# FFN output product of a decoder block: more chunk pairs by seven products, with some of their factors kept in DRAM

## The chip, the cores and the metric

The kernel runs on one core of one Trainium2 chip. The metric is the device time of one execution in microseconds (us). Three runs of the kernel before took 2199.93, 2201.72 and 2203.13 us, so the median is 2201.72 us.

## The reference, cut to what matters

One decoder block on 512 tokens of width 2048 in fp32: an attention mixer (`nsa_mixer`), then a SwiGLU FFN with 5632 hidden columns, then a final RMSNorm. The change touches the last product of the FFN and its neighbours only:

```
def swiglu(h, w_in, w_out):
    z = h @ w_in
    a, b = z[..., :D_FF], z[..., D_FF:]
    return (jax.nn.silu(a) * b) @ w_out
...
        h = h + swiglu(rmsnorm(h, ffn_norm_g[i]), ffn_w_in[i], ffn_w_out[i])
    return rmsnorm(h, final_norm_g)
```

Call `silu(a) * b` the activation A (512 x 5632) and `ffn_w_out` the weights B (5632 x 2048). The kernel computes A B.

## The kernel before, in words

Every fp32 product is made of three matmuls (`three`, L267 to L270): both factors are split into a high part, rounded to the matmul's format, and a low rest. The high part is written by ScalarE (ACT) and the rest by VectorE (DVE); the products high-high, high-low and low-high are accumulated in PSUM.

**The FFN output stage.** The inner dimension 5632 is cut into 22 chunk pairs of 256 (j = 0 to 21) and the 2048 output columns into four blocks of 512 (b = 0 to 3). One step of the stage, a *visit*, is one chunk pair in one block: 4 x 22 = 88 visits, numbered n = 0 to 87 in the order of `ORDER[b]`, block after block. A visit needs the activation of the pair (512 KB, written to DRAM as `d_a` by the stage before) and a 256 x 512 tile of the weights (512 KB).

- A **plain** visit (`plain_tile`) makes 4 token tiles x 2 chunks x 3 = 24 matmuls with 512 columns. It needs the activation loaded (`load_a`) and split (`split_a`) and the weights split.
- A **seven** visit (`seven_unit`) treats the pair as a 2 x 2 block product by seven products (Winograd's form of Strassen's method) instead of eight: 7 products x 2 x 3 = 42 matmuls with 256 columns. On the activation side it needs seven factors (p1 to p7, 128 x 1792 in a high and a low tile, `ah` and `al`, 917,504 bytes each). On the weight side it needs three sums of weight quarters (`weight_sums`: four subtractions or additions on DVE, then a split of 128 x 768).

Before, seven of the 22 pairs are seven visits in every block. Their activation factors are made by `form` at their first visit (in block 0) and stay in SBUF in the pool `asl` for all four blocks. `form` reads the activation from `scratch`, the last quarter of the accumulator `acc`, which is free until block 3. SyncE (SP) loads the next pair to form into it (`load_form`); after the last form, a GpSimd (POOL) DMA puts the residual from `d_r` there.

Four of the seven sums of a block (p1, p5, p6, p7) have PSUM banks of their own (`qs`) and are merged into `acc` by `merge_sums` after the last seven visit of the block.

**What sets the order.** The schedule is manual: each engine executes its instructions in program order. In the loop over visits, iteration n issues, in this order: `prepare(n + 1)` (a form, if visit n + 1 needs one), `W2.take` (the weights of visit n + 1 are split, with the sums if it is a seven visit), `split_a` (the activation of visit n + 1, if plain), the matmuls of visit n, `merge_sums` where due, and one step of `ready`. So DVE does the whole preparation of visit n + 1 in one row. It can't run far ahead: the tiles `thi`/`tlo` (split activation of a plain visit, or split weight sums of a seven visit) have two buffers, so the one for visit n + 1 is free when visit n - 1 has ended on TensorE (PE). The weights have three raw buffers (`RAW`) and four split buffers (`CONV`). The raw activations of plain visits have two single homes, `rawx` and `tt`; `tt` also takes the weight sums.

`ready(b)` runs in block b + 1: at its third visit it issues the load of a 512-column piece of the final norm's gain (`gf`, one buffer, a POOL DMA), and at the next four visits one multiplication of `acc` with `gf` each, on DVE.

The last four visits of block 3 (`N_TAIL`) are done token tile by token tile: all four visits for tile 0, then for tile 1, and so on, with the final norm and the output store behind each tile. Their split activations go to buffers of `asl`, as those come free.

SP's queue carries the loads of weights, of plain activations and of pairs to form; POOL's queue carries `gf` and the loads of `d_r` in this stage.

Of the kernel before, what the change touches and what calls it, by code (L numbers as in the profile page):

```python
# [165 lines left out]
def nsa_block(ctx: ExitStack, tc: tile.TileContext, x, rel_bias, mix_g, ffn_g, fin_g, w_in, w_out,  # L166
# [919 lines left out]
    NU = len(seq)  # L1086
    a_raw, a_hl, seven = {}, {}, {}


    held, free = {}, {"rawx": -1, "tt": -1}  # L1090
    for n, (_, j) in enumerate(seq):
        home = "tt"
        if j not in SEVEN:
            home = min(free, key=free.get)
            held[n] = home, free[home]
        free[home] = n
# [9 lines left out]
    def split_a(n):  # L1106
# [8 lines left out]
        elif n < NU:  # L1115
            a_hl[n] = seven[seq[n][1]]
        load_a(n)
# [3 lines left out]
    def weight_sums(n):  # L1121

        def first(r):
            b11, b12, b21, b22 = (r[:, 256 * i:256 * (i + 1)] for i in range(4))
            ttf = tp.tile([128, 1536], F32, name="tt", bufs=1)[:, :768]
            tt = ttf.rearrange("p (n c) -> p n c", n=3)
            sub(tt[:, 0], b22, b12)
# [4 lines left out]
            def rest():  # L1132
                h, l = (tp.tile([128, 1600], F32R, name=f"t{x}")[:, 32:800] for x in ("hi", "lo"))
                act(h, ttf, AF.Copy)
                sub(l, ttf, f32(h))
                t_hl[n] = [x.rearrange("p (n c) -> p n c", n=3) for x in (h, l)]
# [4 lines left out]

    for n, (_, j) in enumerate(seq):
        if j in SEVEN:
            W2.sums[n] = weight_sums(n)
# [19 lines left out]
    late.tile([128, 16], F32, name="late_gap")  # L1164
    asl = ctx.enter_context(tc.tile_pool(name="asl", bufs=len(SEVEN)))
    late2 = ctx.enter_context(tc.tile_pool(name="late2", bufs=1))
    ss = [late2.tile([128, 4], F32, name=f"sf{t}") for t in range(NT)]
    scratch = acc[:, :, 1536:]
    forms = [j for _, j in seq[:NF // 2] if j in SEVEN]

    def load_form(i):
        if i < len(forms):
            nc.sync.dma_start(scratch[:, :2], d_a[forms[i]].rearrange("p (n c) -> p n c", n=2))
        else:
            pool.dma_start(scratch, d_r[:, :, 1536:].rearrange("t p c -> p t c"))

    def form(j):
# [9 lines left out]
        for c0, c1, src in ((0, 256, a11), (256, 768, a[:, 1]), (768, 1792, m)):  # L1187
# [4 lines left out]
            sub(ol, src, f32(oh))  # L1192
        seven[j] = [x.rearrange("p (n c) -> p n c", n=7) for x in (h, l)]

# [3 lines left out]
    def prepare(n):  # L1198

        j = seq[n][1] if n < NU else None  # L1200
        if n < NF // 2 and j in SEVEN:
            form(j)
            load_form(forms.index(j) + 1)

# [54 lines left out]
    for b in range(4):  # L1259
        units = ORDER[b][:-N_TAIL] if b == 3 else ORDER[b]  # L1260
        po = [pf.tile([128, 512], F32, name=f"f{i}") for i in range(4)]
        qs = {x: pf.tile([128, 512], F32, name=f"f{i}") for i, x in enumerate(("p1", "p5", "p6", "p7"))}
        first7 = next(j for j in units if j in SEVEN)
        last7 = [j for j in units if j in SEVEN][-1]
        started = False
        for i, j in enumerate(units):
# [3 lines left out]
            while na <= n + 1 + max(0, 2 - left):  # L1270
                split_a(na)
                na += 1
            if j in SEVEN:
                seven_unit(n, w, first7)
# [65 lines left out]
```

## Time and profile before

| quantity | value |
|---|---|
| the profiled execution's own time | 2201.19 us |
| its span (first to last instruction) | 2199.4 us |
| median of three runs | 2201.72 us (2199.93 to 2203.13) |
| mean granted TensorE clock | 0.997 |
| PE, PEld, DVE, ACT, POOL busy | 98%, 90%, 69%, 42%, 4% |
| FFN output stage on PE | 1719.6 to 2189.7 us |
| DMA traffic of the whole span | 306.34 MB, mean 139 GB/s |
| seven visits, plain visits | 28, 60 |

How to read it: the profile is one execution, 1.8 us shorter in span than its device time. Busy shares are of the span; PEld is the loading of the stationary operand, beside PE. Window rows of the trace give, for a stretch of the span, the busy time of each engine with its number of instructions in brackets, the granted TensorE clock (1.00 is full), the mean busy share of the 16 DMA engines, and GB/s. In rows of the timeline the columns are start, duration, engine, line, operation, tiles, shape and count; in square brackets stands how long the engine sat idle before it and what released it. Rows of DMA issues give the count, the size and the median us from issue to landing. q1 is the hardware queue that SP's loads use, q0 the software queue of POOL.

### The profile page before, as it was taken

The page shows a single profiled execution, that of the slowest core. Times are in us where ns is not written, and L with a number is a line of the kernel's source. Part 1 is how long each engine was busy: PE and PEld are TensorE (multiplying, and loading weights), DVE is VectorE, ACT ScalarE, POOL GpSimd, SP SyncE. Part 2 cuts the span into 40 slices and gives each one's busy share as a digit, 9 for nine tenths or more (in the row PEclk, how much of TensorE's full clock was granted, in tenths as well). Part 3 has the DMA queues.
Part 4 walks back from the last instruction along what each step waited for, and adds up shares of the span by engine and source line. Part 5 has one row for each costly group of instructions (what it writes and reads, how often), then busy time and mean ns, then how long its engine had stood idle before and what let it go on. Part 6 is the DMA issues. An engine that isn't in the chain of part 4 may idle for free.

```text
span 2199.4 us, 36466 instructions
## 1 busy us (share of the span) xinstructions
PE 2158.3 (98%) x14866; PEld 1990.0 (90%) x14866; DVE 1523.9 (69%) x2458; ACT 929.0 (42%) x1429; POOL 97.4 (4%) x95
## 2 busy tenths in 40 slices
PE   6999999999999999999999999999999999999998
PEld 5889898888989888899999999999999888888886
DVE  5454656656655437798888888888888678566665
ACT  5343444444444324343434434343444344344344
POOL 3100000000013012000000000000000000000000
PEclk9999999999999999999999999999999999999999
DMA  5755233323253543244444334333443655555445
GB/s 167 206 147 158 81 93 91 92 82 97 89 204 115 187 149 116 96 134 126 125 125 134 122 120 125 127 122 126 126 125 125 223 199 196 179 173 166 162 158 182
DMA packets 233496, 306.34 MB, mean 139 GB/s; under 512 B 12367, under 2 KB 178287, under 8 KB 232176
## 3 DMA queue, kind: packets, MB, share of 16 engines
q1 hardware_dynamic: 226016, 273.58, 38.9%
q0 software_dynamic: 6016, 27.29, 3.4%
q10 hardware_dynamic: 1296, 3.15, 0.4%
q8 instruction: 116, 1.90, 0.3%
q14 instruction: 52, 0.43, 0.1%
HBM read 275.56 MB, written 33.66 MB: 141 GB/s over the span
## 4 chain that ended last, share of the span: by engine, by line
PE 94%; DVE 3%; DMA 1%; ACT 1%; issue 0%; SPq 0%; ACTq 0%; DVEq 0%
PE f L269 19%; PE f L268 18%; PE f L270 18%; PE proj L268 8%; PE proj L270 8%; PE proj L269 8%; PE pt L735 2%; PE pp L270 1%; PE pp L269 1%; PE pp L268 1%; PE o L270 1%; PE o L269 1%; PE s L268 1%; PE s L270 1%; PE o L268 1%; PE s L269 1%
## 5 line engine op out<-in xcount | busy, mean ns | idle before, releaser
L92 DVE TENSOR_TENSOR wlo<-raw,whi 128x1024 fp32r<-128x1024 f32 (+1 forms) x208 | 252.5, 1217 | 136.8 <-ACT whi L90 135.9
L90 ACT ACTIVATE whi<-raw 128x1024 fp32r<-128x1024 f32 (+1 forms) x226 | 234.0, 1039 | 156.7 <-DVE raw L890 62.9
L890 DVE TENSOR_TENSOR tlo<-tt,thi 128x1536 fp32r<-128x1536 f32 (+2 forms) x132 | 197.8, 1498 | 141.6 <-ACT thi L992 89.0
L268 PE MATMUL f<-hn_h,whi 128*128 128x256 f32 x984 | 271.7, 276 | 0.7 <-ACT E L950 0.7
L270 PE MATMUL f<-hn_h,wlo 128*128 128x256 f32 x984 | 271.6, 276 | 0.0
L269 PE MATMUL f<-hn_l,whi 128*128 128x256 f32 x984 | 271.6, 276 | 0.0
L987 ACT ACTIVATE whi<-raw 128x1024 fp32r<-128x1024 f32 x123 | 126.1, 1057 | 292.4 <-DVE raw L890 282.1
L268 PE MATMUL proj<-hn_h,whi 128*128 128x512 f32 (+1 forms) x544 | 210.2, 386 | 1.0 <-DVE hn_l L257 1.0
L270 PE MATMUL proj<-hn_h,wlo 128*128 128x512 f32 (+1 forms) x544 | 207.6, 382 | 0.0
L269 PE MATMUL proj<-hn_l,whi 128*128 128x512 f32 (+1 forms) x544 | 207.1, 381 | 0.0
L268 PEld LDWEIGHTS f<-hn_h,whi 128*128 128x128 f32 x984 | 184.7, 188 | 1.1 <-ACT E L950 1.1
L270 PEld LDWEIGHTS f<-hn_h,wlo 128*128 128x128 f32 x984 | 184.7, 188 | 0.0
L269 PEld LDWEIGHTS f<-hn_l,whi 128*128 128x128 f32 x984 | 184.7, 188 | 0.0
L270 PE MATMUL f<-whi,tlo 128*128 128x512 f32 x448 | 175.1, 391 | 1.2 <-DVE tlo L890 1.2
L269 PE MATMUL f<-wlo,thi 128*128 128x512 f32 x448 | 174.9, 390 | 0.0
L268 PE MATMUL f<-whi,thi 128*128 128x512 f32 x448 | 174.6, 390 | 0.0
L992 ACT ACTIVATE thi<-tt 128x1536 fp32r<-128x1536 f32 x82 | 121.8, 1485 | 84.6 <-PE f L269 75.9
L890 DVE TENSOR_TENSOR wlo<-raw,whi 128x1024 fp32r<-128x1024 f32 x123 | 147.0, 1223 | 0.0
L268 PE MATMUL proj<-whi,hn_h 128*128 128x256 f32 (+2 forms) x496 | 146.3, 295 | 0.0
L269 PE MATMUL proj<-wlo,hn_h 128*128 128x256 f32 (+2 forms) x496 | 145.2, 293 | 0.0
L270 PE MATMUL proj<-whi,hn_l 128*128 128x256 f32 (+2 forms) x496 | 145.0, 292 | 0.0
L294 DVE TENSOR_TENSOR ptl<-pt,pth 128x128 fp32r<-128x128 f32 (+3 forms) x128 | 62.4, 488 | 99.1 <-ACT pth L293 98.9
(314 smaller groups left out, 5894.1 us busy)
## 6 DMA issues: line engine op xcount, KB each, us to landing
raw<-in_ffn_w_in SPq DMA_DIRECT2D x135, 512.0 KB, 3.6
raw<-in_ffn_w_out SPq DMA_DIRECT2D x88, 512.0 KB, 4.5
raw<-in_nsa_w_in SPq DMA_DIRECT2D x48, 512.0 KB, 3.6
rawx<-in_ffn_w_in SPq DMA_DIRECT2D x41, 512.0 KB, 4.9
rawx<-d_a SPq DMA_DIRECT2D x36, 512.0 KB, 3.6
raw<-in_nsa_w_out SPq DMA_DIRECT2D x32, 512.0 KB, 3.6
raw<-in_nsa_w_in SPq DMA_DIRECT2D x56, 256.0 KB, 3.3
tt<-d_a SPq DMA_DIRECT2D x24, 512.0 KB, 4.5
```

The costliest lines, as they stand in the source:

```text
L90: self.nc.scalar.activation(hi[:, :n], src, AF.Copy)
L92: eng.tensor_tensor(lo[:, :n], src, hi[:, :n].bitcast(F32), op=OP.subtract)
L268: mm(o, ah, bh, start=start, stop=False, skip_group_check=True)
L269: mm(o, ah, bl, start=False, stop=False, skip_group_check=True)
L270: mm(o, al, bh, start=False, stop=stop, skip_group_check=True)
L294: dve.tensor_tensor(lo, psum_ap, hi.bitcast(F32), op=OP.subtract)
L735: nc.tensor.transpose(pt[rows, 128 * (t - kt):128 * (t - kt + 1)], src, ident)
L890: dve.tensor_tensor(o, a, b, op=OP.subtract)
L987: act(h, r, AF.Copy)
L992: act(h, ttf, AF.Copy)
```

## The change

The set of seven visits now depends on the block. Five pairs, `KEPT` = 3, 8, 13, 17, 19, are seven visits everywhere and keep their factors in SBUF (`asl`, now five buffers of a high and a low tile). Nine more pairs become seven visits from some block on: 5, 10, 15 from block 0; 0, 1, 2, 4 from block 1; 6, 7 from block 2. Their factors are formed once, in a new pool `ast` with two buffers, and used from there; `form` also writes them to DRAM (`d_s`, two POOL DMAs). In each later block they are loaded back into a buffer of `ast` (`load_seven`, two POOL DMAs per visit). In total 48 visits are seven and 40 are plain; 14 pairs are formed, where 7 were.

The visits of the four blocks, numbered n:chunk pair, with p for plain, k for kept, v for passing through `ast`, f where the pair is formed:

```
0:0p 1:1p 2:2p 3:3fk 4:4p 5:5fv 6:6p 7:7p 8:8fk 9:9p 10:10fv 11:11p 12:12p 13:13fk 14:14p 15:15fv 16:16p 17:17fk 18:18p 19:19fk 20:20p 21:21p
22:3k 23:6p 24:5v 25:7p 26:0fv 27:9p 28:8k 29:11p 30:10v 31:12p 32:1fv 33:14p 34:13k 35:16p 36:2fv 37:17k 38:15v 39:18p 40:4fv 41:19k 42:20p 43:21p
44:5v 45:9p 46:3k 47:10v 48:11p 49:6fv 50:12p 51:15v 52:8k 53:14p 54:0v 55:16p 56:13k 57:1v 58:18p 59:7fv 60:17k 61:2v 62:19k 63:4v 64:20p 65:21p
66:5v 67:3k 68:10v 69:9p 70:15v 71:8k 72:0v 73:11p 74:1v 75:13k 76:2v 77:12p 78:4v 79:17k 80:6v 81:19k 82:7v 83:14p 84:16p 85:18p 86:20p 87:21p
```

In the program, the load for a visit stands in the iteration in which its buffer's user is at work, and POOL waits there until that user has ended on PE. From block 2's end on this is two v visits earlier: the load for visit 72 waits for the end of visit 68, and so on to visit 82, which waits for 78. The loads for visits 38, 51 and 61 stand in iterations 35, 48 and 58, right behind a form and its two writes. The last form is that of visit 59, so the load of the residual into `scratch` is now issued in iteration 58 too, between the writes of that form and the load for visit 61. In block 3 the `gf` load is issued in iteration 68, behind the load for visit 72.

The tail's four plain visits now follow only one plain visit (83) after the last seven visit (82), and `merge_sums` of block 3 is issued in iteration 82. Before, five plain visits stood between.

The core of the diff:

```diff
-SEVEN = (3, 6, 9, 12, 14, 17, 19)
-ORDER = [tuple(range(22))] + 2 * [(3, 0, 1, 6, 2, 4, 9, 5, 7, 12, 8, 10, 14, 11, 13, 17, 15, 16, 19, 18, 20, 21)] + [
-    (3, 0, 6, 1, 9, 2, 12, 4, 14, 5, 17, 7, 19, 8, 10, 11, 13, 15, 16, 18, 20, 21)]
+KEPT = (3, 8, 13, 17, 19)
+SEVEN = [KEPT + x for x in ((5, 10, 15), (5, 10, 15, 0, 1, 2, 4)) + 2 * ((5, 10, 15, 0, 1, 2, 4, 6, 7),)]
+ORDER = [tuple(range(22)),
+         (3, 6, 5, 7, 0, 9, 8, 11, 10, 12, 1, 14, 13, 16, 2, 17, 15, 18, 4, 19, 20, 21),
+         (5, 9, 3, 10, 11, 6, 12, 15, 8, 14, 0, 16, 13, 1, 18, 7, 17, 2, 19, 4, 20, 21),
+         (5, 3, 10, 9, 15, 8, 0, 11, 1, 13, 2, 12, 4, 17, 6, 19, 7, 14, 16, 18, 20, 21)]
...
+    d_s = dram.tile([NF // 2, 2, 128, 1792], F32, name="d_s")
...
-            a_hl[n] = seven[seq[n][1]]
+            a_hl[n] = seven[seq[n][1]] if seq[n][1] in KEPT else passing.pop(0)
...
+            c0 = 0 if n and seq[n - 1][1] in SEVEN[seq[n - 1][0]] else 32
...
-                h, l = (tp.tile([128, 1600], F32R, name=f"t{x}")[:, 32:800] for x in ("hi", "lo"))
+                h, l = (tp.tile([128, 1600], F32R, name=f"t{x}")[:, c0:c0 + 768] for x in ("hi", "lo"))
...
-    asl = ctx.enter_context(tc.tile_pool(name="asl", bufs=len(SEVEN)))
+    asl = ctx.enter_context(tc.tile_pool(name="asl", bufs=len(KEPT)))
+    ast = ctx.enter_context(tc.tile_pool(name="ast", bufs=2))
...
-    forms = [j for _, j in seq[:NF // 2] if j in SEVEN]
+    forms = [n for n, (b, j) in enumerate(seq) if j in SEVEN[b] and (not b or j not in SEVEN[b - 1])]
+    visits = [n for n, (b, j) in enumerate(seq) if j in SEVEN[b] and j not in KEPT]
...
-        h, l = (asl.tile([128, 1792], F32R, name=f"a{x}") for x in "hl")
+        h, l = ((asl if j in KEPT else ast).tile([128, 1792], F32R, name=f"a{x}") for x in "hl")
...
+        if j not in KEPT:
+            for i, x in enumerate((h, l)):
+                pool.dma_start(d_s[j, i], x.bitcast(F32))
+        keep_seven(j, h, l)
...
+    def load_seven(n):
+
+        while n_visit[0] < len(visits):
+            v = visits[n_visit[0]]
+            if v in forms or sum(x > n for x in visits[:n_visit[0]]) >= 2:
+                break
+            h, l = (ast.tile([128, 1792], F32R, name=f"a{x}") for x in "hl")
+            for i, x in enumerate((h, l)):
+                pool.dma_start(x.bitcast(F32), d_s[seq[v][1], i])
+            keep_seven(seq[v][1], h, l)
+            n_visit[0] += 1
...
+        if n in forms:
+            form(seq[n][1])
+            load_form(forms.index(n) + 1)
+            n_visit[0] += n in visits
...
+            load_seven(n)
             if i >= 2:
                 next(todo, None)
```

More of the change, by code (lines that the diff above doesn't have):

```diff
@@ L1086, in nsa_block @@
     NU = len(seq)
-    a_raw, a_hl, seven = {}, {}, {}
+    a_raw, a_hl, seven, passing = {}, {}, {}, []
     held, free = {}, {"rawx": -1, "tt": -1}
-    for n, (_, j) in enumerate(seq):
+    for n, (b, j) in enumerate(seq):
         home = "tt"
-        if j not in SEVEN:
+        if j not in SEVEN[b]:
             home = min(free, key=free.get)
@@ L1140, in weight_sums @@
         return first
-    for n, (_, j) in enumerate(seq):
-        if j in SEVEN:
+    for n, (b, j) in enumerate(seq):
+        if j in SEVEN[b]:
             W2.sums[n] = weight_sums(n)
@@ L1192, in form, with keep_seven @@
             sub(ol, src, f32(oh))
-        seven[j] = [x.rearrange("p (n c) -> p n c", n=7) for x in (h, l)]
+        if j not in KEPT:
+            for i, x in enumerate((h, l)):
+                pool.dma_start(d_s[j, i], x.bitcast(F32))
+        keep_seven(j, h, l)
+    def keep_seven(j, h, l):
+        x = [x.rearrange("p (n c) -> p n c", n=7) for x in (h, l)]
+        if j in KEPT:
+            seven[j] = x
+        else:
+            passing.append(x)
+    n_visit = [0]
+    def load_seven(n):
[8 more added lines that the diff above has]
+            n_visit[0] += 1
     pool.dma_start(acc[:, :, :1536], d_r[:, :, :1536].rearrange("t p c -> p t c"))
@@ L1198, in prepare @@
     def prepare(n):
[L1200 to L1203, printed above, removed]
+        if n in forms:
+            form(seq[n][1])
+            load_form(forms.index(n) + 1)
+            n_visit[0] += n in visits
     def plain_tile(n, w, t, first, last):
@@ L1262, in nsa_block @@
         qs = {x: pf.tile([128, 512], F32, name=f"f{i}") for i, x in enumerate(("p1", "p5", "p6", "p7"))}
-        first7 = next(j for j in units if j in SEVEN)
-        last7 = [j for j in units if j in SEVEN][-1]
+        first7 = next(j for j in units if j in SEVEN[b])
+        last7 = [j for j in units if j in SEVEN[b]][-1]
         started = False
```

4 lines of the change are left out of this document (2 added, 2 removed).

## The prediction, on record before the run

> **What bounds the kernel now.** First the page, then the chain of waits, then the stage by windows.
>
> ```profile
> span 2199.4 us, 36466 instructions
> PE 2158.3 (98%) x14866; PEld 1990.0 (90%) x14866; DVE 1523.9 (69%) x2458; ACT 929.0 (42%) x1429; POOL 97.4 (4%) x95
> PE 94%; DVE 3%; DMA 1%; ACT 1%; issue 0%; SPq 0%; ACTq 0%; DVEq 0%
> 1720.00:1740.00 20.00, 19.36 (x97) 16.00 (x97) 16.66 (x24) 8.85 (x11) 1.28 (x2) 1.00 0.83 311
> 1740.00:1760.00 20.00, 17.50 (x90) 14.56 (x89) 14.20 (x19) 9.59 (x11) 0.00 (x0) 0.94 0.61 221
> 1760.00:2140.00 380.00, 380.00 (x2215) 335.70 (x2214) 254.28 (x327) 160.59 (x187) 2.94 (x5) 1.00 0.53 178
> 1754.97 0.38 PE L268 MATMUL f<-thi,ah 128*128 128x256 f32 x1 [0.96 <-ACT thi L1134]
> 1756.37 0.38 PE L269 MATMUL f<-tlo,ah 128*128 128x256 f32 x1 [1.01 <-DVE tlo L890]
> 1758.00:1762.00 4.00, 4.00 (x24) 4.00 (x24) 1.72 (x2) 0.00 (x0) 0.00 (x0) 0.60 0.86 288
> ```
>
> PE is the bound, 94% of the chain. In the output stage it is idle for 0.64 and 2.50 us in the first 40 us and then works 380 of 380 us. DMA stands at 178 GB/s there. One thing to remember: after two waits of about 1 us at 1755, the granted clock was 0.60 over the next 4 us, which costs about 4 x 0.4 = 1.6 us more.
>
> **The gain on PE.** Exact windows of one seven visit and of two plain ones:
>
> ```profile
> 1841.71:1846.56 4.85, 4.85 (x43) 1.00 0.76 242
> 1846.56:1857.49 10.93, 10.93 (x51) 1.00 0.63 208
> 1650.00:1700.00 50.00, 50.00 (x443) 50.00 (x442) 44.70 (x53) 20.90 (x20) 1.07 (x2) 1.00 0.39 127
> ```
>
> A seven visit takes 4.85 us, a plain one 10.93 / 2 = 5.465. The change turns 20 plain visits into seven visits: 20 x 0.615 = **-12.3 us**. Seven visits in a row (block 3) cost no more: in the stage before, 443 matmuls of 256 columns ran in 50 us, 0.113 us each, against 4.85 / 42 = 0.115 here.
>
> **What DVE gets.** One preparation with form, one without:
>
> ```profile
> 1816.70 1.23 DVE L890 TENSOR_TENSOR tlo<-rawx,thi 128x1024 fp32r<-128x1024 f32 x1 [0.22 <-ACT thi L1112]
> 1817.85 0.42 DVE L893 TENSOR_TENSOR acc<-acc 128x256 f32<-128x256 f32 x1
> 1821.67 0.42 DVE L890 TENSOR_TENSOR tt<-raw 128x256 f32<-128x256 f32 x1
> 1824.82 0.95 DVE L890 TENSOR_TENSOR tlo<-tt,thi 128x768 fp32r<-128x768 f32 x1
> 1836.47 0.42 DVE L890 TENSOR_TENSOR tt<-raw 128x256 f32<-128x256 f32 x1
> 1839.63 0.95 DVE L890 TENSOR_TENSOR tlo<-tt,thi 128x768 fp32r<-128x768 f32 x1
> L1254 DVE TENSOR_TENSOR acc<-acc,gf x12: 683/684/686, 1859.7 to 2106.7; 128x512 f32<-128x512 f32 x12
> ```
>
> A form takes 1817.85 to 1821.67 = 3.8 us, the weights of a seven visit 1836.47 to 1840.58 = 4.1, a plain preparation two splits of about 1.15, a `gf` step 0.68. Seven visits in a row need 4.1 (4.8 with a `gf` step) of 4.85 us: hidden. For seven, plain, formed seven, the plain split ends 2.3 us after the first seven visit s starts (its `thi` is free only then: 1815.6 to 1817.9), so the formed one is ready at s + 2.3 + 3.8 + 4.1 = 10.2, and PE wants it at 10.3. Fits by 0.1 us; every lateness shows. Visit 49 has a `gf` step ahead of its form: 0.6 us late. Forms 15 and 17 stand two visits apart while 15's factors are being written; the scratch load has 10.3 - 3.8 = 6.5 us, I take 0.5 late (0 to 1.5). The start of block 0 (form 5 where form 6 was) waits for the same 3 MB load; I take no difference (-4 to +4, its whole loss on either side). The shifted column `c0` changes no shape: nothing, to 0.1 us each way.
>
> **What DMA gets.**
>
> ```profile
> 1730.00:1734.00 4.00, 4.00 (x19) 3.30 (x19) 3.74 (x8) 1.67 (x2) 0.00 (x0) 1.00 1.02 415
> 1738.00:1742.00 4.00, 4.00 (x36) 3.89 (x34) 0.00 (x0) 1.08 (x2) 0.00 (x0) 1.00 1.02 393
> q1 hardware_dynamic: 1616, 3.64, 48.1%
> q0 software_dynamic: 672, 3.67, 44.5%
> acc<-d_r POOLq DMA_DIRECT2D x1, 3072.0 KB, 15.6
> raw<-in_ffn_w_out SPq DMA_DIRECT2D x5, 512.0 KB, 9.0
> DMA packets 32921, 78.55 MB, mean 179 GB/s; under 512 B 2421, under 2 KB 2421, under 8 KB 32891
> d_a<-E POOLq DMA_DIRECT2D x22, 512.0 KB, 2.9
> d_r<-acc POOLq DMA_DIRECT2D x4, 1024.0 KB, 4.2
> acc<-d_r POOLq DMA_DIRECT2D x1, 1024.0 KB, 5.6
> gf<-in_final_norm_g POOLq DMA_DIRECT2D x1, 256.0 KB, 6.0
> 1822.05 0.78 POOL L1175 DMA_DIRECT2D acc<-d_r  x1 [96.25 <-DVE al L890]
> 1822.81 0.55 POOL L1249 DMA_DIRECT2D gf<-in_final_norm_g  x1
> ```
>
> Saturated, DMA moves 393 to 415 GB/s; I take 400. The writes 2.9 us for 512 KB and 4.2 for 1024 KB give 1.6 us fixed. A pair's factors are 2 x 917,504 B = 1.835 MB. Added: 9 writes 16.5 MB, 19 reloads 34.9, 7 more scratch loads 3.7; removed: 20 plain loads 10.5. So 78.6 + 44.6 = 123 MB in some 440 us, 280 GB/s: it fits on average, and what counts is each deadline. Steady in block 3: a reload has three visits, 15.2 us, for 1.7 + 1.835 MB / 270 GB/s (400 less SP's 130) = 8.5 us: hidden by the three visits; without that cover each of nine would be up to 8.5 late.
>
> *Visit 61.* The form for 59 ends 6.1 us after 57 starts, 1.25 after 58 does; its high part can be written 1.2 us earlier, near the start of 58. Behind it in POOL's queue: the low part, the 1.05 MB residual, the reload: 4.72 MB. SP's own 2.1 MB in that time leave 276 GB/s: 17.1 us, landing 0.1 + 1.6 + 17.1 = 18.8. PE wants 61 after 5.46 + 4.85 + 4.85 = 15.2: **3.6 late** (2 to 7, by 320 and 230 GB/s).
>
> *Visits 38 and 51.* Two writes and a reload, 3.67 MB, beside 2.5 MB of SP's: 6.2 / 0.4 = 15.4 + 1.7 = 17.1 against 15.2: **1.9 late** for 38 (0 to 3); 51 has one more plain visit but the late form: **1.9** with the 0.6 at 49 (0 to 3).
>
> *Visit 71, a new wait.* POOL, in order, waits for the end of visit 68 to reload 72, and `gf` for block 3 stands behind it, in POOL's program and in q0. DVE's first `gf` step waits for that, and behind it on DVE stands the weight preparation of 71, for which PE waits. 1.835 + 0.26 MB at 270 GB/s land 1.7 + 7.8 = 9.5 us after 68 ends; then 0.7 + 4.1, makes 14.3; PE wants 71 after 5.46 + 4.85 = 10.3: **4.0 late** (2.5 to 5). That q0 works in order is seen at 1822: the 1 MB load landed at 1822.05 + 5.6 = 1827.7, `gf`, issued 0.8 us behind it, at 1828.8, though it is a quarter of the size. There, `gf` was issued 37 us before its first use at 1859.7.
>
> **The tail.** The merge now stands right before it.
>
> ```profile
> 1828.22 0.60 ACT L1236 ACTIVATE m<-f 128x512 f32<-128x512 f32 x1 [1.22 <-PE f L270]
> 1830.77:1841.71 10.94, 10.94 (x50) 1.00 0.52 190
> 1832.95 1.22 DVE L893 TENSOR_TENSOR acc<-acc,m 128x1024 f32<-128x1024 f32 x1
> 2166.30 0.32 SPq L1104 DMA_DIRECT2D rawx<-d_a  x1
> 2169.75 1.06 ACT L1112 ACTIVATE ah<-rawx 128x1024 fp32r<-128x1024 f32 x1 [0.89 <-DMA rawx<-d_a]
> 2170.84 1.22 DVE L890 TENSOR_TENSOR al<-rawx,ah 128x1024 fp32r<-128x1024 f32 x1 [0.72 <-ACT ah L1112]
> ```
>
> In block 0 the seven visit ended at 1830.77 and its merge at 1834.17, 3.4 later; now a split stands before it, so T + 4.4, with T the end of visit 82. Then DVE splits the weights of 85 and 86 and the activation of 85, done at T + 7.8. Only then is `rawx` free for visit 87: landing 3.45 later (2166.30 to 2169.75), high part T + 12.3, low part T + 13.6. PE does 83 (5.46) and three quarter visits of 1.37 and wants 87 at T + 9.6; with 0.5 us at 85 and the low part wanted 0.45 us after the high one, **3.6 late** (2.5 to 5).
>
> **The clock.** Waits of 3.6 and 4.0 us should bring the drop seen at 1758 twice: 3.3 (0 to 7, nearer to the two that are longer than the two waits at 1755 together).
> In the Trainium skill, "TensorE: Matmul & The Clock Gate", Part 1, the clock is halved after an idle window of about 3.4 us; in this trace two waits of 1 us were enough, so the measurement is the harsher one.
>
> **Sum.** 3.6 + 1.9 + 1.9 + 0.5 + 4.0 + 3.6 + 3.3 = 18.8 lost, 12.3 won: +6.5 on the profiled 2201.2 (span 2199.4 and 1.8 around it) = 2207.7. The median of the runs is 0.5 above the profiled time: **2208.2**. All lower ends: 7 lost, -5, 2196; all upper ends with block 0's 4: 35, +23, 2225.
>
> **Rivals.**
> *Not slower: POOL's queue gets more than what SP leaves.* Place: the reloads of 38, 51, 61, 72. A row of factors is 7,168 B, one of weights 2,048; if the two queues take turns row by row, POOL gets 0.78 of 400 = 311 GB/s. Then 61 lands at 1.7 + 15.2 = 16.9, 1.7 late; 38 and 51 on time but for the 0.6 at 49; 71 is 2.9 late; the tail and 0.5 stay; one clock drop: 11.0 lost, 2199.9, or 2200.4 as a median. It decides from about 300 GB/s. Against it: in the saturated stretch q0 moved 3.67 MB beside 3.64, though its packets were 2.4 times as large.
> The Trainium skill, "DMA: Bandwidth & Descriptors", Queues, rings and completion order, has the engines go round the queues by packets, which would favour this rival; the equal bytes here don't show it.
>
> *Faster: most waits are covered*, since DVE, ACT and SP reach these places earlier than I assume; only the tail stays: 2201.7 - 12.3 + 4 = 2193. For it: 440 us at 280 of 400 GB/s leave room. Against: POOL's waits for the end of a visit are in the program, and `gf` did land behind the load.
>
> *Worse: SP's loads come late too.* In the saturated 20 us of block 0, weights took 9.0 us to land and the stage lost 6 us with the clock. Three such stretches (38, 51, 61) at 6 each, with 71, the tail and a drop (4.0 + 3.6 + 1.7): 27, +15: 2217.
>
> *It doesn't do what it says*: seven visits in a row run slower; excluded by the 443 above, 2 in 100.
>
> **Chances.** Forecast 50, POOL's larger share 20, covered 12, worse 16, the last 2. Range: **2194 to 2221**. A difference below 0.2% (4.4 us) can't be told from none here. Slower by more: the forecast but its lowest part (43), worse and the last: 61. Within: 7 + 18 = 25. Faster: 14.
>
> **What would show it.** Seven visits at 4.85 us, 48 of them. PE waits on an `ah`/`al` load at 61, smaller at 38 and 51; a DVE wait for gf's DMA in block 3 and PE's wait for `tlo` behind it; in the tail, ACT waiting for `rawx` and PE for ACT and DVE; clock below 1 after each. Wrong if PE stays at 100% through blocks 1 to 3, or if waits sit on `wlo` everywhere.

## The result, and the profile after

The changed kernel takes 2228.95 us (median of four runs, 2224.97 to 2231.84). The kernel before took 2201.66 us on the same chip (four runs, 2199.93 to 2203.13). The ratio is 1.0123, 95% interval 1.0104 to 1.0142: slower by 27 us, where 6.5 were predicted. The profiled execution is the fastest of the four, 2224.97 us, with a span of 2223.1 us; it is read against the 2201.19 us of the profiled run before, 23.8 us apart. No trace shows the other 4 us of the median.

The page after, the lines that answer to those shown of before, and the line of POOL's queue (packets, MB, share of 16 engines):

```profile
span 2223.1 us, 37421 instructions
PE 2159.1 (97%) x15226; PEld 2004.1 (90%) x15226; DVE 1573.6 (71%) x2587; ACT 937.9 (42%) x1450; POOL 127.2 (6%) x151
q0 software_dynamic: 14080, 78.67, 9.1%
PE 83%; DVE 6%; DMA 5%; issue 3%; ACT 2%; POOL 0%; SPq 0%; ACTq 0%; DVEq 0%; POOLq 0%
```

The averages hardly move: PE falls from 98 to 97%, DVE rises from 69 to 71%. The chain tells more. PE held 94% of it, now 83%, and DMA 5% where it had 1%. The three windows of the output stage (busy us of PE, PEld, DVE, ACT, POOL; clock; DMA share; GB/s):

```profile
1720.00:1740.00 20.00, 19.37 (x96) 15.94 (x96) 17.22 (x25) 8.92 (x11) 1.28 (x2) 1.00 0.73 264
1740.00:1760.00 20.00, 17.35 (x109) 15.49 (x108) 12.39 (x18) 7.81 (x9) 1.07 (x2) 0.91 0.93 327
1760.00:2140.00 380.00, 361.33 (x2332) 326.90 (x2331) 286.40 (x423) 162.36 (x200) 27.74 (x52) 0.98 0.74 270
```

The first 40 us are as they were (0.63 and 2.65 us idle, where it was 0.64 and 2.50). In the 380 us behind them PE, which had worked all 380, is idle for 18.7 us. DMA moves 270 GB/s there, near the 280 predicted and far below the 393 to 415 of the prediction's full windows; the whole span moves 350.97 MB, 44.6 more than before, as added up. So the new idle time lies in the middle, while the average load is as foreseen. The waits of PE name it (total us, times, longest):

```profile
PE f L272 <- ACT thi L1139: 7.0, 4, 4.2
PE f L273 <- DVE tlo L894: 5.3, 8, 1.0
PE f L274 <- DMA al<-d_s: 3.7, 2, 3.3
PE f L272 <- ACT thi L1116: 3.6, 1, 3.6
...
PE f L272 <- ACT ah L1116: 2.0, 1, 2.0
```

One long wait each stands behind a weight split (`thi`, L1139), a reload (`al<-d_s`) and a plain activation (`thi`, L1116), and one in the tail (`ah`, L1116).

For the account by place I took the starts of the visits on PE from its timeline, and from each stretch its visits at 5.465 us (plain) or 4.846 (seven). What is left is lost: waits, and the slow clock after them. Before, the stage lasted from 1719.61 to 2189.65 = 470.0 us; 60 plain and 28 seven visits make 463.6; lost 6.4. After, it lasted from 1722.43 to 2213.44 = 491.0; 40 and 48 make 451.2; lost 39.8. So the gain of 12.4 us is there, and 33.4 us of new loss. The last 2.8 us of the 23.8 are a later start of the stage, behind code that the change doesn't touch; over the kernels of this study that start lies between 1717.7 and 1726.0, so below I compare what is lost, not spans.

| visits | lost, us | what PE waits for at first | predicted, with the clock |
|---|---|---|---|
| 0 to 5 | 6.0 | split weights and activation of the start | as before (6.1) |
| 8, 12 to 13, 29 | 3.4 | `tlo`, `thi` | 0 |
| 18 to 19 | 5.2 | `tlo` and `thi` behind a late `rawx` | 0.5 |
| 36 to 38 | 0.5 | `al` of the reload | 1.9 |
| 42 to 43 | 5.8 | `thi` from a late `tt` | 0 |
| 49, 51 | 0.8 | `tlo` at 49, none at 51 | 1.9 |
| 59 to 63 | 5.4 | `al` of the reload for 61 | 3.6 + 1.65 |
| 70 to 72 | 8.0 | `thi` behind the `gf` step | 4.0 + 1.65 |
| 83 to 87 | 4.0 | `ah` of 87 | 3.6 |

(The rest, 0.7, lies in places below 0.6 each.) Of 14.6 us that were not foreseen, most are at 18 to 19 and 42 to 43, 11.0 us together. The timeline around 18 (start, duration, engine, line):

```profile
1804.78 0.53 POOL L1202 DMA_DIRECT2D d_s<-ah  x1 [26.22 <-ACT ah L1198]
1806.04 0.53 POOL L1202 DMA_DIRECT2D d_s<-al  x1 [0.73 <-DVE al L894]
1807.15 0.53 POOL L1222 DMA_DIRECT2D al<-d_s  x1
...
1812.47 0.34 SPq L1108 DMA_DIRECT2D rawx<-d_a  x1
...
1824.38 1.06 ACT L1116 ACTIVATE thi<-rawx 128x1024 fp32r<-128x1024 f32 x1 [3.02 <-DMA rawx<-d_a]
```

SP's load of the activation for visit 18 was issued at 1812.47 and used at 1824.38, 11.9 us later, where such a load mostly took 3.6 before. What stands ahead of it is in POOL's queue: the two writes of pair 15 and, right behind them, the reload for visit 24, nine iterations before its due time. Visits 8 and 12 to 13 are of the same kind, but with a write alone on POOL's queue: ACT waits 6.2 and 5.4 us for SP's load into `tt`.

```profile
1761.48 1.06 ACT L1116 ACTIVATE thi<-tt 128x1024 fp32r<-128x1024 f32 x1 [6.16 <-DMA tt<-d_a]
...
1789.49 1.06 ACT L1116 ACTIVATE thi<-tt 128x1024 fp32r<-128x1024 f32 x1 [5.37 <-DMA tt<-d_a]
```

Around 43 there is a write with reloads again:

```profile
1940.99 0.54 POOL L1202 DMA_DIRECT2D d_s<-ah  x1 [18.36 <-ACT ah L1198]
...
1942.78 0.53 POOL L1222 DMA_DIRECT2D ah<-d_s  x1
...
1950.14 0.34 SPq L1108 DMA_DIRECT2D tt<-d_a  x1
...
1951.21 0.53 POOL L1222 DMA_DIRECT2D ah<-d_s  x1 [7.37 <-PE f L274]
...
1963.78 1.06 ACT L1116 ACTIVATE thi<-tt 128x1024 fp32r<-128x1024 f32 x1 [6.94 <-DMA tt<-d_a]
```

Two writes, the reload for 44 and, at 1951, the one for 47; SP's load is 13.6 us under way and ACT stands 6.9 us for it. How the queues share the core's DMA in such stretches (queue: packets, MB, share of the engines' time), first 1940 to 1964, then 2043 to 2064, where visit 61 is late:

```profile
q0 software_dynamic: 939, 5.75, 58.1%
q1 hardware_dynamic: 1381, 3.20, 38.7%
...
q0 software_dynamic: 979, 5.61, 71.8%
q1 hardware_dynamic: 624, 1.45, 18.5%
```

POOL's q0 has 5.75 of 8.95 MB, 64%, in the first and 5.61 of 7.06, 79%, in the second. SP's need does not come first: in the second, PE and DVE stand for POOL's reload and for SP's weights.

```profile
2060.38 0.43 DVE L894 TENSOR_TENSOR tt<-raw 128x256 f32<-128x256 f32 x1 [2.45 <-DMA raw<-in_ffn_w_out]
...
2063.30 0.38 PE L274 MATMUL f<-thi,al 128*128 128x256 f32 x1 [3.33 <-DMA al<-d_s]
```

All loads into `tt` in this stage, before and after (from issue to landing, lowest, median, highest):

```profile
DMA to landing us min/median/max: 4.2/4.5/9.5
```

```profile
DMA to landing us min/median/max: 4.3/7.6/13.5
```

### The profile page after: what moved, and what is told of

It reads as the page before. It is cut to its first block, busy times and chain, and to the rows that moved or that the text cites. A ratio compares the mean times of both kernels' runs of the same rounds, so it can differ in the third digit from the quotient of the medians.

```text
span 2223.1 us, 37421 instructions
## 1 busy us (share of the span) xinstructions
PE 2159.1 (97%) x15226; PEld 2004.1 (90%) x15226; DVE 1573.6 (71%) x2587; ACT 937.9 (42%) x1450; POOL 127.2 (6%) x151
## 2 busy tenths in 40 slices
DMA packets 240588, 350.97 MB, mean 158 GB/s; under 512 B 13055, under 2 KB 178975, under 8 KB 239264
## 3 DMA queue, kind: packets, MB, share of 16 engines
q0 software_dynamic: 14080, 78.67, 9.1%
## 4 chain that ended last, share of the span: by engine, by line
PE 83%; DVE 6%; DMA 5%; issue 3%; ACT 2%; POOL 0%; SPq 0%; ACTq 0%; DVEq 0%; POOLq 0%
PE f L273 15%; PE f L274 15%; PE f L272 15%; PE proj L272 8%; PE proj L274 8%; PE proj L273 8%; PE pt L739 2%; DMA tt<-d_a 2%; DVE tlo L894 1%; DMA rawx<-d_a 1%; PE pp L274 1%; PE o L274 1%; PE pp L273 1%; PE pp L272 1%; PE o L273 1%
## 5 line engine op out<-in xcount | busy, mean ns | idle before, releaser
L272 PE MATMUL f<-whi,ah 128*128 128x256 f32 (+1 forms) x416 | 120.6, 290 | 2.0 <-ACT ah L1116 2.0
L274 PEld LDWEIGHTS proj<-hn_h,wlo 128*128 128x128 f32 x544 | 103.9, 191 | 19.8
L274 PE MATMUL f<-whi,al 128*128 128x256 f32 (+1 forms) x416 | 120.5, 290 | 1.1 <-DVE al L894 1.1
```

The source lines that it names most:

```text
L272: mm(o, ah, bh, start=start, stop=False, skip_group_check=True)
L274: mm(o, al, bh, start=False, stop=stop, skip_group_check=True)
```

## The experiments

The theory that I formed from this, here A: the round trip through DRAM is the whole loss, and mostly by SP's own loads, which come late beside POOL's bursts. The first rival, B: DVE and ACT are too full with 48 seven visits, whatever DMA does. The second, C: only the reloads themselves, and the `gf` load behind one, come too late. All medians below have the kernel before beside them on the same chip; "lost" is the account by place of the profiled run.

### Without the round trip, and each half alone

`e1_no_roundtrip` writes nothing and reloads nothing; visits that would use reloaded factors use those of pair 3.

```diff
-        if j not in KEPT:
-            for i, x in enumerate((h, l)):
-                pool.dma_start(d_s[j, i], x.bitcast(F32))
...
-            h, l = (ast.tile([128, 1792], F32R, name=f"a{x}") for x in "hl")
-            for i, x in enumerate((h, l)):
-                pool.dma_start(x.bitcast(F32), d_s[seq[v][1], i])
-            keep_seven(seq[v][1], h, l)
+            passing.append(seven[KEPT[0]])
```

> Leaves out the round trip of the nine pairs through DRAM: no writes, no reloads; the v visits that would use reloaded factors use those of pair 3 (wrong numbers, same matmuls). Forms, weight sums, order and PE work are those of the changed kernel. Theory A (the loss comes from POOL's writes and reloads, which make SP's loads of plain activations and weights late): the losses at visits 8, 13, 18/19, 29, 42/43, 49, 60/61 and the gf wait at 71 go, 30 us in the profile; left are block 0's start (about 5) and the tail (4): 2192 to 2198. Theory B (DVE and ACT are too full with forms and sums): the losses stay, 2215 or more. Theory C (only the reloads' own deadlines and gf): 61 and 71 go (13 us), the rest stays: 2208 to 2213.

Measured: 2198.06 us (2194.31 to 2201.16), ratio 0.9979, interval 0.9968 to 0.9990. The stage lost 15.4 us: 8.2 at the start, 0.9 at 49, 0.7 at 59 to 63, 5.5 in the tail. Its middle, with the columns as above:

```profile
1760.00:2140.00 380.00, 379.28 (x2566) 348.80 (x2565) 307.93 (x457) 172.13 (x209) 2.37 (x4) 1.00 0.51 162
```

The time is at the upper edge of A's 2192 to 2198. PE works 379.28 of 380 us, though DVE has more to do than in any other of these kernels (307.93 us). B falls for the middle: DVE and ACT keep up. The round trip is the new idle time of the middle. What stays without it is a start and a tail.

`e2_writes_only` keeps the writes and drops the reloads; `e3_reloads_only` writes pair 5 alone and loads its factors for all.

The core of e2:

```diff
-            h, l = (ast.tile([128, 1792], F32R, name=f"a{x}") for x in "hl")
-            for i, x in enumerate((h, l)):
-                pool.dma_start(x.bitcast(F32), d_s[seq[v][1], i])
-            keep_seven(seq[v][1], h, l)
+            passing.append(seven[KEPT[0]])
```

The core of e3:

```diff
-        if j not in KEPT:
+        if j == 5:
...
-                pool.dma_start(x.bitcast(F32), d_s[seq[v][1], i])
+                pool.dma_start(x.bitcast(F32), d_s[5, i])
```

> Leaves out the reloads only (v visits behind a form use the factors of pair 3); the nine pairs are still written to DRAM. Theory A: each write of 1.835 MB still delays SP's loads for some 8 us, so 8 and 13 (2.7 us) and part of 18/19 and 42/43 stay: 2197 to 2205. Theory C: no loss from writes, 2192 to 2197.

> Leaves out eight of the nine pairs' writes; every reload reads the factors of pair 5 (wrong numbers, same bytes and rows). Theory A: the reloads in a burst (24 behind form 15; 44 and 47 behind form 40) still take DMA from SP, so part of 18/19 and of 42/43 stays, 61 shrinks to 0 to 3 since 1.8 MB ahead of its reload are gone, 71 stays (8): 2208 to 2220. Theory C: only 71 and the tail stay: 2203 to 2208.

Measured: e2 2201.96 us (ratio 1.0000, 0.9990 to 1.0010), lost 17.4; e3 2206.19 us (1.0015, 1.0006 to 1.0024), lost 22.9. The middle of e2, then of e3:

```profile
1760.00:2140.00 380.00, 376.37 (x2523) 344.35 (x2522) 303.44 (x448) 171.51 (x210) 11.44 (x21) 1.00 0.62 206
```

```profile
1760.00:2140.00 380.00, 372.12 (x2471) 340.72 (x2470) 300.21 (x443) 169.71 (x208) 21.25 (x40) 0.99 0.70 247
```

Idle there: none to speak of without either (0.7), 3.6 with the writes, 7.9 with the reloads, 18.7 with both. In neither of the two is anything lost at 18 to 19 or 42 to 43, and at 59 to 63 no more than 0.7; e2 lost 2.1 at 6 to 8 and 1.9 at 12 to 13, e3 lost 2.3 at 6 to 8, where it still writes pair 5, nothing at 12 to 13, and 8.6 at 70 to 72. So 8 and 12 to 13 need a write only, and 18 to 19 and 42 to 43 need both: a write with a reload right behind it. That corrects A: it had part of these two places stay with either half, and for e3 2208 to 2220. The measured 2206.19 lies in C's 2203 to 2208, but C has no reason for ACT's waits for SP's loads at 18 and 43 in the changed kernel. With the reloads alone the load for visit 18 lands before ACT asks for it:

```profile
1809.42 0.34 SPq L1108 DMA_DIRECT2D rawx<-d_a  x1
1817.40 1.06 ACT L1116 ACTIVATE thi<-rawx 128x1024 fp32r<-128x1024 f32 x1 [0.62 <-ACT whi L93]
```

ACT waits for its own step `whi`, not for the load. One place needs the reloads alone: 70 to 72, the `gf` load.

### Smaller rows

If the queues took turns packet by packet, smaller rows for POOL would give SP more. `e4_rows_1792` keeps the factors in rows of 1,792 B in DRAM, where they had 7,168.

```diff
-    d_s = dram.tile([NF // 2, 2, 128, 1792], F32, name="d_s")
+    d_s = dram.tile([NF // 2, 2, 4, 128, 448], F32, name="d_s")
...
-                pool.dma_start(d_s[j, i], x.bitcast(F32))
+                pool.dma_start(d_s[j, i].rearrange("k p c -> p k c"), x.bitcast(F32).rearrange("p (k c) -> p k c", k=4))
...
-                pool.dma_start(x.bitcast(F32), d_s[seq[v][1], i])
+                pool.dma_start(x.bitcast(F32).rearrange("p (k c) -> p k c", k=4), d_s[seq[v][1], i].rearrange("k p c -> p k c"))
```

> The factors lie in DRAM in four pieces, so a row of POOL's writes and reloads is 1,792 bytes instead of 7,168; bytes, order and waits are the same. Theory A with a share by rows (POOL's queue took 79% of the bytes beside SP's at visit 60 because its rows are longer): SP's loads land sooner, 18/19 and 42/43 shrink from 11 us to under 5 together, while reloads land later and PE waits for them at 38, 51, 61 and 71 (each 2 to 6 more): 2215 to 2232 with the waits at other places, and q0's bytes at most equal to q1's where both are busy. If the row length doesn't matter: the same places and sizes as in the changed kernel, 2225 to 2232.

Measured: 2232.45 us (1.0128, 1.0108 to 1.0147), lost 49.4: every place of the table is there, with 5.7 at 17 to 19, 7.5 at 42 to 43, 7.3 at 59 to 63. SP got no more. Its queues from 1940 to 1964:

```profile
q0 software_dynamic: 1122, 5.39, 59.0%
q1 hardware_dynamic: 1313, 3.02, 40.4%
```

q0 has 5.39 of 8.41 MB, 64%, as in the changed kernel, though its packets are smaller: 5.39 MB / 1122 = 4.8 KB, where they were 5.75 / 939 = 6.1 KB. That is a cut by a fifth and not to a quarter (over the whole program q0 has 16,768 packets for 14,080), so this was a weak test of the size; it shows that POOL's share did not follow such a cut. The Trainium skill, "DMA: Bandwidth & Descriptors", Queues, rings and completion order, says that each DMA engine goes round its queues and drains a packet from one before it turns to the next. If the packets that the trace counts are these, then with one of each in turn, and both queues always having work, the counts would be equal; they are 939 to 1381 and 979 to 624 in the two stretches of the changed kernel, and q0 has 64 and 79% of the bytes. The rule alone gives neither the counts nor the shares, and no run shows that both queues had work all the time.

### The places one by one

`e5_gf_early` issues the `gf` load 14 iterations earlier, in the block before; `e6_residual_late` takes the residual out of POOL's queue between form 59 and the reload for 61 and issues it at visit 64; `e7_spread` lets no reload be issued more than four visits ahead, and paces POOL by a one-column copy of the weights just split.

The core of e5:

```diff
+            if b < 3 and i == 10:
+                load_gf(b)
...
-        gf = late2.tile([128, 512], F32, name="gf")
-        pool.dma_start(gf, fin_g[None, c].to_broadcast([128, 512]))
+        gf = gfs.pop(b)
```

The core of e6:

```diff
-        else:
-            pool.dma_start(scratch, d_r[:, :, 1536:].rearrange("t p c -> p t c"))
...
+            if n == 64:
+                pool.dma_start(scratch, d_r[:, :, 1536:].rearrange("t p c -> p t c"))
```

The core of e7:

```diff
-            if v in forms or sum(x > n for x in visits[:n_visit[0]]) >= 2:
+            if v in forms or sum(x > n for x in visits[:n_visit[0]]) >= 2 or v - n > 4:
                 break
+            paced(w)
```

> One edit: the load of gf for the next block is issued at the eleventh visit of the block before, ahead of the reloads, instead of behind the reload for visit 72. Theory (POOL's order makes DVE wait for gf, and PE for DVE): the 8.0 us at visit 71 (5.7 of waits and the clock drop behind them) fall to 0 to 1, all other places stay: 2218 to 2224. Rival (the DMA is full there, so weights or the reload are late instead): 4 us or more stay at 70 to 72, 2225 or above.

> One edit: the 1 MB residual load that stood between the writes of visit 59's factors and the reload for 61 is issued six visits later. Theory (61 is late by the bytes ahead of its reload): at 316 GB/s, what POOL got there, the reload lands 3.3 us earlier and the loss in visits 59 to 63 falls from 5.4 to 0 to 2 with the clock drop gone: 2223 to 2227. Rival (weights are late there by themselves): 4 or more stay.

> Reloads are issued at most four visits ahead of their use, and POOL is held to that by a one-column copy of the weights of the visit at work. So the reload for 24 no longer follows the writes at visit 14, nor those for 44 and 47 the writes at 39; all bytes stay. Theory A' (not the writes, not the reloads, but a write with reloads right behind it keeps DMA full so long that SP's single-buffered activation loads come late): 18/19 falls from 5.2 to under 1, 42/43 from 5.8 to under 2, the rest stays: 2215 to 2224. Rival (total bytes): these losses turn up at other visits, 2226 or more.

Measured, each against the 39.8 lost and the 2228.95 us of the changed kernel:

| kernel | median, us | ratio (95%) | lost | its place, after its edit |
|---|---|---|---|---|
| e5 | 2215.61 | 1.0060 (1.0045 to 1.0075) | 30.8 | 70 to 72: 8.0 to 0 |
| e6 | 2222.44 | 1.0097 (1.0080 to 1.0114) | 36.4 | 59 to 63: 5.4 to 0.7 |
| e7 | 2218.05 | 1.0069 (1.0051 to 1.0087) | 34.1 | 18 to 19: 5.2 to 0; 42 to 43: 5.8 to 0 |

Each edit clears its place, which shows its cause. At 18 to 19 the loss is 0 in all kernels that hold the reload back (e7 and, below, e9, e10 and e12); only e5 has less there without that, 2.0. At 61 it is the sum of what stands ahead of the reload: e6 takes 1 MB of it away, e3 took the 1.8 MB of the write, and either leaves 0.7. The intervals of e6 and of the changed kernel overlap a little; those of e5 and e7 don't. Of `gf`, the changed kernel's rows first, then e5's:

```profile
2105.28 0.53 POOL L1222 DMA_DIRECT2D ah<-d_s  x1 [9.04 <-PE f L274]
2105.79 0.53 POOL L1222 DMA_DIRECT2D al<-d_s  x1
...
2106.32 0.54 POOL L1280 DMA_DIRECT2D gf<-in_final_norm_g  x1
...
2116.27 0.69 DVE L1285 TENSOR_TENSOR acc<-acc,gf 128x512 f32<-128x512 f32 x1 [9.25 <-DMA gf<-in_final_norm_g]
```

```profile
2102.52 0.68 DVE L1290 TENSOR_TENSOR acc<-acc,gf 128x512 f32<-128x512 f32 x1
```

`gf` was issued at 2106.32 behind 1.8 MB of reload and DVE stood 9.25 us until 2116.27; with the early load DVE's step has no wait in front. Its landing isn't faster: in e5, too, each early `gf` load stands right behind writes or a reload and takes 9.1 to 11.5 us, where the kernel before has 3.7 to 6.0. What the edit gives it is 14 visits in which to land.

```profile
DMA to landing us min/median/max: 9.1/10.4/11.5
```

There is a price: in block 0 it stands behind the writes of pair 10, and e5 lost 5.2 at 12 to 13 (1.9 before its edit). A load that is moved meets something else.

Of e7, the places that it clears come to 11.0 us and its median is 10.9 lower, while the loss of its profiled run, the slowest of four, is lower by only 5.7. It lost 3.9 at 6 to 8 (0.9 in the changed kernel). But its edit changes nothing before visit 14: there this is a difference between executions. The changed kernel, e5, e6, e7 and e8 are one program up to visit 9, and their profiled runs lost 6.9, 6.9, 6.4, 8.7 and 7.4 us in visits 0 to 8; at 59 to 63, which the edits of e5 and e8 don't touch, these two lost 2.8 and 3.9, not 5.4. So 2 us at one place, between two profiles, prove little; 5 to 8 us that fall to nothing are well beyond that.

### The tail

`e8_tail` puts the last merge behind the first token tile of the tail and gives the activations of visits 86 and 87 homes of their own in the free `ast` buffers, so that they can be loaded before `rawx` is free.

```diff
+            if n >= NU - 2:
+                held[n] = "ast", 80
+                continue
...
-            if j == last7:
+            if j == last7 and b < 3:
...
+        if t == 0:
+            merge_sums(3)
```

> The merge of block 3 is issued behind the first token tile of the tail instead of at visit 82, and the plain activations of the last two visits are loaded into a free buffer of the pool for passing factors. Theory (the merge on DVE delays the split of 85 and so the load for 87): the tail's 4.0 us fall to 0 to 1: 2224 to 2228. Rival (weights of 87, which need the buffer of visit 83, set it): 3 or more stay.

Measured: 2228.61 us (1.0119, 1.0099 to 1.0140), no gain. PE's loss in the tail went from 4.0 to 3.4, but what follows PE's last matmul grew: from 2223.1 - 2213.4 = 9.7 us to 2230.7 - 2218.1 = 12.6. The merge on DVE was only pushed behind, into the norm of the tiles, where DVE is the last engine to work. And weights are late at the tail's start; SP now issues two activation loads just ahead of them, at 2177:

```profile
2185.39 1.06 ACT L93 ACTIVATE whi<-raw 128x1024 fp32r<-128x1024 f32 x1 [6.28 <-DMA raw<-in_ffn_w_out]
```

So the theory's 0 to 1 us was missed, and the rival's sign came: 3 or more left with weights late, though not those of 87. e12 below has the two homes with the merge in its old place, and there PE waits in the tail for DVE (`wlo`, `al`) and not for `rawx`. So taking the wait for `rawx` away doesn't help, since DVE with the merge is late behind it.

### All that paid, together

`e9_four_edits` has the edits of e5 to e8. `e10_acc_late` has these four too, and cuts the 3 MB load of the accumulator at the stage's start into four pieces of a token tile each and issues them at visits 6, 8, 11 and 12; `e11_before_acc_late` is the kernel before with that one edit. `e12_best` has the edits of e5 to e7, of e8 only the two homes, the accumulator's load cut by blocks (one piece at the start, two at visits 20 and 45), and another choice of labels: written pairs 3, 8, 13 in block 0, each with one plain visit behind it, kept pairs 5, 10, 15, 17, 19.

The core of e10 (e11 has the same, with the copy of `paced` written out):

```diff
-    pool.dma_start(acc[:, :, :1536], d_r[:, :, :1536].rearrange("t p c -> p t c"))
...
+            if n in (6, 8, 11, 12):
+                t = (6, 8, 11, 12).index(n)
+                paced(w)
+                pool.dma_start(acc[:, t, :1536], d_r[t, :, :1536])
```

The core of e12:

```diff
-KEPT = (3, 8, 13, 17, 19)
+KEPT = (5, 10, 15, 17, 19)
...
+            if n in (20, 45):
+                paced(w)
+                c = slice(512 * (b + (n == 20)), 512 * (b + (n == 20)) + 512)
+                pool.dma_start(acc[:, :, c], d_r[:, :, c].rearrange("t p c -> p t c"))
```

> The four edits together: gf ahead of the reloads, the residual load six visits later, reloads at most four visits ahead of use, the tail's merge and homes. Theory (the waits are separate and add up): of the 40 us that the stage loses, 18/19 and 42/43 (11), 61 (4 to 5) and 71 (8) go and the tail gives about 1; left are 14 to 17: 2200 to 2207, within 0.3% of the kernel before. Rival (what is taken away at one place returns at the next, since the bytes stay): 2210 or more.

> As the four edits, and the 3 MB load of the accumulator, which fills DMA at the start of block 0, is cut into four pieces and issued at visits 6, 8, 11 and 12. Theory (the start's 5 us, which the kernel before loses as well, come from that load): 4 to 6 less than the four edits alone, 2195 to 2202, if its pieces don't meet the writes of visits 10 and 15; if they do, nothing gained.

> The kernel before with only that load cut and moved. It tells what of the last kernel's time is the change's and what this load's: 4 to 6 us below the kernel before, 2196 to 2198, by the theory; no difference if its start waits for something else.

> The changed kernel with the edits that paid, put together anew: gf loaded early; the residual piece of the visit after the last block merge three visits later; reloads at most four visits ahead; the tail order of the changed kernel with only the two homes of visits 86 and 87 changed; the first accumulator loads cut into three pieces, one at the start, the others at visits 20 and 45; and the chunk pairs labelled so that each written pair is followed by one plain visit only. What writes and reloads move in bytes is unchanged. Theory (the loss is made of SP's and POOL's loads that come late where a write and reloads meet; each place can be cleared by itself): start of the stage 1 to 3 us lost, visits 8 and 13 under 1 each, 18 to 19, 42 to 43, 59 to 63 and 70 to 72 under 1 each, tail 1.5 to 3.5, sum 10 to 16: 2193 to 2202 us, 0 to 0.4% faster than before. Rival (the bytes decide: 51 MB more must come through and a wait cleared in one place comes back in another): sum 20 or more as in the two kernels before, 2206 to 2214 us, still slower than before.

| kernel | median, us (lowest to highest) | ratio (95%) | lost |
|---|---|---|---|
| e9 | 2214.03 (2208.17 to 2217.42) | 1.0046 (1.0031 to 1.0062) | 26.4 |
| e10 | 2211.58 (2210.85 to 2214.32) | 1.0048 (1.0035 to 1.0060) | 22.5 |
| e11 | 2203.31 (2200.30 to 2205.72) | 1.0001 (0.9992 to 1.0010) | 5.2 |
| e12 | 2201.94 (2198.53 to 2209.15) | 0.9999 (0.9989 to 1.0009) | 22.0 |

e9 lost 18 to 19, 42 to 43, 61 and 70 to 72 to nothing or below 1, 23.7 us in all, but other places got 10.3 worse: it now loses 5.0 at 11 to 13, as e5 does, 3.8 at 54 to 55, 2.2 at 38. It also has e8's late merge, 12.6 us behind PE's last matmul where the changed kernel has 9.7. At 2214.03 the rival's forecast held (2210 or more) and not the theory that the waits add up (2200 to 2207): the four edits, one by one, had lowered the median by 31 us in sum; together they lower it by 15. e10, whose time against before is that of e9, brings the start down to 1.1 and loses 4.1 at 6 to 8 and 6.5 at 11 to 13, where its pieces meet the write of pair 10. e11, without any round trip, shows the same on a small scale: the start's 6.4 turn into 3.9 at 7 to 9, and the time is that of before. A burst can be moved; something must be found that it doesn't meet.

e12 found most of it. Its middle, and its two largest waits in the tail:

```profile
1760.00:2140.00 380.00, 375.78 (x2498) 343.01 (x2498) 299.50 (x443) 169.85 (x208) 43.35 (x79) 1.00 0.81 292
```

```profile
PE f L271 <- DVE al L891: 1.8, 1, 1.8
PE f L270 <- DVE wlo L92: 1.8, 1, 1.8
```

PE idles 4.2 us in the middle where the changed kernel idles 18.7, with the same bytes and 292 GB/s. Visits 8 and 13, 18 to 19 and 70 to 72 lose nothing to speak of, 42 to 43 lose 1.2, 36 to 38 1.3. But the start lost 8.3 and the tail 6.5, of 22.0. The profiled run took 2208.02 us, 6 above the median; whether a typical run loses as much in these two isn't known. The median is at the upper edge of what the theory gave and below the rival's; the sum of the profiled run is on the rival's side. By time, then: e12 is 27 us faster than the changed kernel and level with the kernel before. No kernel here that does the whole work beats the kernel before; e1, which leaves the round trip out, beats it by 0.2%, and that is the ceiling of this plan as long as start and tail are what they are.

## Why the prediction was wrong

By its own steps:

- **The gain** (-12.3): right. The ideal of the visits fell from 463.6 to 451.2 us. That e1 got only 4.3 of them (2202.35 - 2198.06) is the tail's 5.5, where before lost less than 0.4, and 2.1 more at the start and 1.6 in the blocks.
- **DVE fits by 0.1 us**: right; e1 has DVE at 307.93 of 380 us with PE at 379.28.
- **Block 0's start, no difference**: right, 6.0 where it was 6.1, though in part by luck: e5 to e8, the same program there, lost 4.8 to 6.2.
- **Visits 38 and 51** (1.9 each): 0.5 and 0, and 0.8 at 49. Too high, because POOL's queue gets more than what SP leaves: from 1919.8 to 1935.1, for 38, its 3.67 MB ran beside 1.65 MB of SP's, where 2.5 were set. That was the first rival's mechanism, and it was right in it, but not in its time (2200.4), since it left SP's side out too.
- **Visit 61** (3.6, and a clock drop): the wait was 3.3, and 5.4 are lost in all. The size came out, in part by luck: from POOL's first issue there, at 2045.25, to 2064 its queue moved 5.61 MB, 300 GB/s where 276 were put down, but part of that was the reload for 63, issued at 2054.98, which isn't in the sum. SP moved 1.45 MB where 2.1 were set, and its weights took 12.2 us (median of four) to land. That the bytes ahead of the reload are the cause is shown by e6 and e3.
- **Visit 71** (4.0, and a clock drop): waits of 4.2 and 0.8, together the upper end of its 2.5 to 5, and 8.0 in all; e5 shows the cause. The clock cost more than the 1.65 put down.
- **The tail** (3.6): 4.0; but by e8 and e12 DVE with the merge would be late even with a free home for 87, so the home is only part of the reason.
- **The clock** (3.3): low. Behind both waits it stood at half to two thirds for a while. The waits at 71, and the clock around the waits at 61 and 71:

```profile
2119.63 0.58 PE L272 MATMUL f<-thi,ah 128*128 128x256 f32 x1 [4.23 <-ACT thi L1139]
2121.03 0.58 PE L273 MATMUL f<-tlo,ah 128*128 128x256 f32 x1 [0.81 <-DVE tlo L894]
...
2064.00:2068.00 4.00, 4.00 (x24) 4.00 (x23) 1.07 (x3) 0.00 (x0) 0.00 (x0) 0.57 1.01 406
...
2119.00:2123.00 4.00, 2.56 (x10) 2.26 (x11) 3.93 (x7) 1.79 (x4) 0.00 (x0) 0.50 0.91 355
2121.00:2125.00 4.00, 3.97 (x18) 3.97 (x19) 3.60 (x7) 2.59 (x5) 0.00 (x0) 0.50 0.57 210
2123.00:2127.00 4.00, 4.00 (x26) 4.00 (x26) 3.67 (x5) 2.76 (x5) 0.00 (x0) 0.68 0.39 135
```

- **The step that failed** is the one that says of visit 61 "SP's own 2.1 MB in that time leave 276 GB/s", and of a steady reload "400 less SP's 130". It takes SP's need as served first. Then only POOL's deadlines can be missed, and only they were looked at. In the runs SP's need isn't met first, POOL's bursts take 64 to 79% of the bytes, and SP's single-buffered loads pay: 18 to 19 (5.2), 42 to 43 (5.8), 8, 12 to 13 and 29 (3.4) make 14.4 us, and the gap between the 39.8 lost and the 25.2 foreseen (18.8, and 6.4 as before) is 14.6. The other errors cancel: 70 to 72 cost 2.4 more, 38, 49 and 51 2.5 less, the tail 0.4 more. The prediction's own row spoke against the step: in the full 20 us of block 0 the queues moved equal bytes (3.67 and 3.64 MB), and SP's weights took 9.0 us.

The rival "SP's loads come late too" had this mechanism, with 16 chances in 100, and 15 us for it, but put it at 38, 51 and 61, where the reload is urgent. It came where a reload is *not* urgent (18 and 43): the program issues it as soon as a buffer is free, right behind a write; and at 8 and 13 behind a write alone. e2 and e3 show that 18 and 43 need both, e7 that they are clear when the reload is held back.

What stays open: why q0 had 79% of the bytes at 61 and only half in the saturated 20 us of block 0 shown in the prediction (e4 cut the packets by a fifth only; that SP, with one buffer each, has fewer loads waiting there than POOL was not tried); and whether e12's start and tail cost as much in a typical run as in the profiled one.

## What to carry to other kernels

Where two DMA queues share the engines, don't give one of them its need first: list, for every burst on one queue, the loads of the other that are in flight in it, and compare their buffers' slack with a landing time three to four times as long (here 13.5 and 14.5 us for 4.5 and 3.6). A prefetch that isn't due is not free: issue it by its due time, not by the moment that its buffer is free, above all behind a write. And read what stands behind a large transfer in an in-order queue: 256 KB took 9.9 us here, and issuing them 14 visits earlier cleared the 8 us of their place. Last, what single edits gain needn't add up: try them together before counting on the sum.

## What the runs showed of the hardware

- POOL's software queue is not served behind SP's: 5.61 MB against 1.45 in 21 us at 2043, 5.75 against 3.20 in 24 us at 1940. With rows cut to 1,792 B the packets fell to 4.8 KB on average, not to 1.8, and the share stayed at 64%.
- A load of 512 KB that took 3.6 to 4.5 us (medians of `rawx` and `tt` before) took up to 14.5 and 13.5 us beside a write and reloads, while DMA moved 402 GB/s in all (2000 to 2015) and 374 (1940 to 1964).
- With waits of 4.2 and 0.8 us, PE's clock was 0.50 from 2119 to 2125 and 0.68 over the 4 us from 2123; the waits are 5.0 us and the place lost 8.0.
- A 256 KB load on POOL's queue took 3.7 to 6.0 us in the kernel before and 9.1 to 11.5 in e5, where each stands behind 1.8 MB of writes or reload.
